# Gate and up products by seven block products for eight, down product in four phases

## Chip, cores and metric
The kernel runs on one NeuronCore of one Trainium2 chip. The metric is the device time of one execution, in microseconds (us); lower is better. TensorE multiplies, VectorE, ScalarE and GpSimd work elementwise, and the sync engine (SP) issues the DMA transfers.

## The reference
Two pre-norm layers, each a feed-forward block, a mixer (pooling and dilated attention) and a second feed-forward block, are followed by a third, different mixer and a fifth feed-forward block. Everything is float32, with 512 tokens, width 1024 and inner width 2816. Only the five feed-forward blocks change:

```python
def rmsnorm(x, g):
    xf = x.astype(jnp.float32)
    y = xf * lax.rsqrt(jnp.mean(xf * xf, axis=-1, keepdims=True) + NORM_EPS)
    return (y * g.astype(jnp.float32)).astype(x.dtype)

def swiglu(h, w_gate, w_up, w_down):
    return (jax.nn.silu(h @ w_gate) * (h @ w_up)) @ w_down
...
for l in range(DEPTH):
    x = x + 0.5 * swiglu(rmsnorm(x, ffn1_norm[l]), ffn1_w_gate[l], ffn1_w_up[l], ffn1_w_down[l])
    ...  # mixer
    x = x + 0.5 * swiglu(rmsnorm(x, ffn2_norm[l]), ffn2_w_gate[l], ffn2_w_up[l], ffn2_w_down[l])
```

## The kernel before
The residual `x` lies transposed in SBUF, eight tiles of 128 features by 512 tokens. Each float32 operand of a product is split into a high part, rounded to the fast format `float32r` by ScalarE (`ACT.activation(..., AF.Copy)`), and a low part, the remainder, which VectorE subtracts. `mm3` (line 255) then makes one 128-deep product of three matmuls: high by high, high by low, low by high (lines 257 to 259). Weights come in units of up to 128x1024, 512 KB: `load_unit` (line 224) issues the transfer from SP, `split_unit` (line 230) makes the high part `wh` (line 235) and the low part `wl` (line 237), and `unit()` keeps this two units ahead of the product. Raw and split tiles have three buffers each.

A feed-forward block is `ffn` (line 370). The activations are the split pairs `yh`, `yl` of the eight x tiles times the norm's gain (`split`, lines 293 and 294). The factor of the norm per token is taken out of the product: `square` adds up the squares (ScalarE, then GpSimd or VectorE, line 306), `row_factor` and `spread` make the factor `rbc`. For each of 22 blocks of the inner width, `one()` makes a gate block and an up block, 8 `mm3` of 512 columns each; `gate` (lines 376 to 384) scales both by `rbc` on VectorE, takes Silu on ScalarE, multiplies, and splits the result into `ah`, `al`. After all 22, the down product makes the eight x tiles one after another, 22 `mm3` each, and line 404 adds each to x and calls `nxt`, which prepares the next stage's pair. `two_first` makes the first two blocks of a layer with the last of the eight x tiles at the end, since it is the one that comes last.

Around the layers stand the mixers. The end of a mixer is `out_part(4, second)`: eight output tiles of 12 matmuls, each added to x and squared; `second` splits the first four tiles at once, and the last four are split behind the loop (lines 786 and 1250). The third mixer scales its output by a row factor first, through the tile `bt` (lines 1226 and 1227).

The order of instructions on each engine is set at build time: a list scheduler goes by the order of the program text and takes a later instruction first where an earlier one isn't ready by its own estimate. On the chip each engine then runs its list in order. Tiles of a pool that is opened in a `with` block lie where those of the pool closed before lay. The kernel has eight PSUM banks: six for products, two for transposes and row factors.

## Time and profile before

| | us |
|---|---|
| median of 3 runs | 2586.91 (2584.3 to 2588.48) |
| the profiled execution | 2587.41 |
| its span, first to last instruction | 2585.6 |
| TensorE busy in it | 2533.5 |
| VectorE busy in it | 1351.1 |
| mean granted clock of TensorE | 0.994 of full speed |

The profiled execution is one run with the hardware profiler on. An engine's busy time is the sum of its instructions; matmuls overlap in it, so the pace of a stream of matmuls is read from the starts in the timeline, not from their durations.

### The profile page before, as it was taken

Reading aid. Unit: us, or ns where it says so; the run is one execution under the profiler, and the core shown is the slowest. Engines: PE = TensorE matmul, PEld = TensorE weight load, DVE = VectorE, ACT = ScalarE, POOL = GpSimd, SP = SyncE. Lnnn points to the kernel's source line nnn. Section 1 sums busy time; section 2 is a strip of 40 time slices with the busy share of each in tenths; the row PEclk is TensorE's granted clock in tenths of the full one; section 3 lists DMA queues with packets and bytes.
Section 4 is the critical chain, followed back from the end, with each engine's and each line's share of the span. In section 5 each row is a group of like instructions: output and inputs, shape, how many; then the busy total and the mean of one; then the engine's idle time right before and its main releaser. Section 6 shows DMA issues by size and latency. Waiting matters only on the chain.

```text
span 2585.6 us, 31298 instructions
## 1 busy us (share of the span) xinstructions
PE 2533.5 (98%) x12114; PEld 2111.0 (82%) x12114; DVE 1351.1 (52%) x2235; ACT 1012.4 (39%) x1615; POOL 343.8 (13%) x498
## 2 busy tenths in 40 slices
PE   8999999999999999999999999999999999999997
PEld 6888888888888888888888888888887887788886
DVE  6444334786444334444336786444337787644423
ACT  4333223674333223332224674333235775432221
POOL 1000004431000000000004431000003553100000
PEclk9999999999999999999999999999999999999999
DMA  4333332112333333333332112333332311233332
GB/s 146 95 96 97 95 110 87 53 41 78 96 97 98 96 99 92 97 98 94 99 109 82 42 44 88 97 98 96 97 108 89 101 42 42 90 98 98 94 98 70
DMA packets 67542, 229.19 MB, mean 89 GB/s; under 512 B 8896, under 2 KB 9280, under 8 KB 67392
## 3 DMA queue, kind: packets, MB, share of 16 engines
q1 hardware_dynamic: 67392, 227.18, 29.0%
q8 instruction: 95, 1.56, 0.2%
q14 instruction: 55, 0.45, 0.1%
HBM read 225.06 MB, written 2.10 MB: 88 GB/s over the span
## 4 chain that ended last, share of the span: by engine, by line
PE 88%; DVE 6%; ACT 3%; issue 2%; POOL 1%; DMA 0%; SPq 0%; DVEq 0%; ACTq 0%; POOLq 0%
PE mm L257 27%; PE mm L259 27%; PE mm L258 27%; PE ov L751 1%; PE tp L733 1%; DVE wl L237 1%; PE mm L490 1%; PE mm L491 1%; PE ov L1030 1%; DVE qk L470 1%; ACT wh L235 1%; PE tp L1002 0%; DVE yl L294 0%; POOL win L610 0%; DVE qk L484 0%
## 5 line engine op out<-in xcount | busy, mean ns | idle before, releaser
L235 ACT ACTIVATE wh<-wr 128x1024 fp32r<-128x1024 f32 (+2 forms) x431 | 447.8, 1040 | 1218.5 <-PE mm L258 685.8
L257 PE MATMUL mm<-yh,wh 128*128 128x512 f32 x2008 | 787.7, 393 | 8.6 <-ACT wh L235 7.1
L258 PE MATMUL mm<-yl,wh 128*128 128x512 f32 x2008 | 783.7, 391 | 1.6 <-DVE yl L294 1.6
L259 PE MATMUL mm<-yh,wl 128*128 128x512 f32 x2008 | 783.1, 390 | 0.5 <-DVE wl L237 0.5
L237 DVE TENSOR_TENSOR wl<-wr,wh 128x1024 fp32r<-128x1024 f32 (+2 forms) x419 | 507.7, 1213 | 399.0 <-ACT wh L235 398.4
L257 PEld LDWEIGHTS mm<-yh,wh 128*128 128x128 f32 x2008 | 377.8, 188 | 85.6 <-ACT wh L235 7.1
L258 PEld LDWEIGHTS mm<-yl,wh 128*128 128x128 f32 x2008 | 378.0, 188 | 80.8 <-DVE yl L294 4.2
L259 PEld LDWEIGHTS mm<-yh,wl 128*128 128x128 f32 x2008 | 377.6, 188 | 79.4 <-DVE wl L237 1.2
L257 PE MATMUL mm<-ah,wh 128*128 128x512 f32 x880 | 342.3, 389 | 0.0
L258 PE MATMUL mm<-al,wh 128*128 128x512 f32 x880 | 342.3, 389 | 0.0
L259 PE MATMUL mm<-ah,wl 128*128 128x512 f32 x880 | 342.3, 389 | 0.0
L306 POOL TENSOR_TENSOR ss<-ss,sq 128x512 f32<-128x512 f32 x48 | 70.8, 1475 | 1726.0 <-ACT sq L305 1703.4
L379 DVE TENSOR_TENSOR t<-mm,rbc 128x512 f32<-128x512 f32 x110 | 76.1, 692 | 341.7 <-PE mm L259 341.7
L376 DVE TENSOR_TENSOR t<-mm,rbc 128x512 f32<-128x512 f32 x110 | 76.1, 692 | 235.7 <-PE mm L259 234.2
L258 PEld LDWEIGHTS mm<-al,wh 128*128 128x128 f32 x880 | 165.2, 188 | 34.4
L257 PEld LDWEIGHTS mm<-ah,wh 128*128 128x128 f32 x880 | 165.2, 188 | 34.4
L259 PEld LDWEIGHTS mm<-ah,wl 128*128 128x128 f32 x880 | 165.2, 188 | 34.1
L257 PE MATMUL mm<-wh,yh 128*128 128x256 f32 (+2 forms) x544 | 183.4, 337 | 1.0 <-DVE vhl L501 1.0
L259 PE MATMUL mm<-wh,yl 128*128 128x256 f32 (+2 forms) x544 | 176.0, 324 | 0.0
L258 PE MATMUL mm<-wl,yh 128*128 128x256 f32 (+2 forms) x544 | 175.7, 323 | 0.1
L257 PEld LDWEIGHTS mm<-wh,yh 128*128 128x128 f32 x544 | 104.1, 191 | 10.0 <-DVE vhl L501 1.9
L258 PEld LDWEIGHTS mm<-wl,yh 128*128 128x128 f32 x544 | 104.2, 192 | 8.6 <-DVE wl L237 0.5
(292 smaller groups left out, 2561.3 us busy)
## 6 DMA issues: line engine op xcount, KB each, us to landing
wr<-in_w SPq DMA_DIRECT2D x388, 512.0 KB, 3.5
wr<-in_w SPq DMA_DIRECT2D x40, 384.0 KB, 3.0
x<-in_xT SPq DMA_DIRECT2D x8, 256.0 KB, 5.8
out<-x SPq DMA_DIRECT2D x8, 256.0 KB, 2.0
bias<-in_consts SPq DMA_DIRECT2D x2, 448.0 KB, 4.2
wr<-in_w SPq DMA_DIRECT2D x2, 420.0 KB, 3.5
ws<-in_ws SPq DMA_DIRECT2D x2, 256.0 KB, 4.2
wr<-in_w SPq DMA_DIRECT2D x1, 280.0 KB, 2.8
```

Of the source, the lines that this page charges most:

```text
L235: ACT.activation(h[:, :n], r[:, :n], AF.Copy)
L237: state["low"] = eng.tensor_sub(l[:, :n], r[:, :n], h[:, :n].bitcast(F32)).ins
L257: PE.matmul(o, w[0], xx[0], start=start, stop=False)
L258: PE.matmul(o, w[0], xx[1], start=False, stop=False)
L259: PE.matmul(o, w[1], xx[0], start=False, stop=stop)
L306: eng.tensor_add(sums["s"], sums["s"], sq)
L376: V.tensor_mul(t1, g, rb)
L379: V.tensor_mul(t2, u, rb)
L470: return V.tensor_sub(dst, src, h.bitcast(F32))
L490: PE.matmul(o, q[g][:, cq], k[g][:, ck], start=True, stop=False)
L491: PE.matmul(o, q[g][:, cq], k[2 + g][:, ck], start=False, stop=True)
L733: PE.transpose(o[:, i * P : (i + 1) * P], prob[h * TC + i][0][:, j * P : (j + 1) * P], ident)
```

## The change
The inner width is taken in 11 pairs of 128-wide blocks. For each pair, with gate and up side by side in one weight tile of 1024, the product is a 2x2 block product: two halves of the depth (four x tiles each), two blocks of the inner width, two halves of the tokens (256 each). Instead of eight block products it makes seven (`PRODUCTS`), each 2 x 4 x 3 matmuls of 256 columns. Four of the seven weight tiles are sums (S1 to S4) that VectorE makes from raw tiles; on the side of x, `prep_a` makes a difference of token halves, and `prep_b` three further combinations. S2, S3 and W22 accumulate over W11's bank and S4 over S1's, with snapshots by ScalarE in between. `evac_act` and `evac` put the blocks together, and `finish` makes scaling, Silu, product and split of a block in three steps, spread over later products by `rest_of`. The pairs come in four phases of 2, 3, 3 and 3; the down product of a phase's blocks, eight pieces, is spread among the next phase's products, and each piece is added to x. The last phase's pieces come at the end, in the order 0, 4, 1, 5, 2, 6, 3, 7. The layer's pool holds weight buffers of its own, `wq` and `wd`, beside `wr`; it opens behind a mixer, where `layers` runs `prep_b` four times, and stays open from the second to the third layer. PSUM's six banks become three tags of two.

```diff
-DOWN = ((0, 8), (8, 8), (16, 6))
+PRODUCTS = ("W11", "S1", "S2", "W12", "S3", "S4", "W22")
+BLOCKS = {"W11": ((0, 0),), "S1": ((1, 0), (1, 1)), "W12": ((0, 1),)}
+PHASES = ((0, 1), (2, 3, 4), (5, 6, 7), (8, 9, 10))
+D_ORDER = (0, 4, 1, 5, 2, 6, 3, 7)
...
+        def source(j):
...
+            if name == "S1":
+                g["21"], g["22"] = m, m + 1
+                t = g["s1"] = state["ffn"].tile([P, 1024], F32, name="wt", tag="wt", bufs=2)
+                V.tensor_add(t, raws[m], raws[m + 1])
+                return t, 1024, []
+            if name == "S2":
+                t = g["s2"] = state["ffn"].tile([P, 1024], F32, name="wt", tag="wt", bufs=2)
+                V.tensor_add(t, g["s1"], raws[g["11"]])
+                return t, 1024, []
...
+            if name == "S3":
+                t = raws[g["21"]]
+                V.tensor_add(t, t, raws[g["11"]])
+                return t, 1024, [g["11"], g["21"]]
+            if name == "S4":
+                t = raws[g["12"]]
+                V.tensor_add(t, t, g["s2"])
+                return t, 1024, [g["12"]]
+            return raws[g["22"]], 1024, [g["22"]]
...
+        def prep_a(c, g):
+            t = small.tile([P, S], F32, name="sq", tag="sq", bufs=2)
+            ACT.activation(t, x[c], AF.Copy, scale=gain(g, c))
+            V.tensor_sub(t[:, HALF:], t[:, :HALF], t[:, HALF:])
+            h, l = new_pair(c)
+            ACT.activation(h, t, AF.Copy)
+            V.tensor_sub(l, t, h.bitcast(F32))
+
+        def prep_b(c, g):
+            b = state["ffn"].tile([P, 4, HALF], F32, name="b4", tag="cc", bufs=2)
+            r = state["ffn"].tile([P, 4, HALF], F32, name="r3", tag="cc", bufs=2)[:, :3]
+            ACT.activation(b[:, 0:2], x[c + 4], AF.Copy, scale=gain(g, c + 4))
+            ACT.activation(b[:, 2:4], x[c], AF.Copy, scale=gain(g, c))
+            V.tensor_sub(r[:, 1], b[:, 1], b[:, 3])
+            V.scalar_tensor_tensor(r[:, 0], r[:, 1], -1.0, b[:, 2], op0=ALU.mult, op1=ALU.subtract)
+            V.scalar_tensor_tensor(r[:, 2], r[:, 0], -1.0, b[:, 0], op0=ALU.mult, op1=ALU.subtract)
...
+            ACT.activation(h, r, AF.Copy)
+            yh, yl = new_pair(c + 4)
+            ACT.activation(yh, b[:, 0:2], AF.Copy)
+            V.tensor_sub(l, r, h.bitcast(F32))
+            V.tensor_sub(yl, b[:, 0:2], yh.bitcast(F32))
...
+            def evac(t, o):
+                if len(t) == 2:
+                    d = t[1]
                     V.scalar_tensor_tensor(x[d], o, coef, x[d], op0=ALU.mult, op1=ALU.add)
-                    nxt(d)
+                    if t[0] == len(PHASES) - 1:
+                        nxt(d)
+                    return
+                _, p, n = t
+                if n == "W12":
+                    V.tensor_add(flat(chunk(2 * p), 0), o[n], snap["W11"])
+                elif n == "S3":
+                    V.scalar_tensor_tensor(flat(chunk(2 * p + 1), 1), o[n], -1.0, snap["S1"], op0=ALU.mult, op1=ALU.subtract)
+                elif n == "S4":
+                    V.tensor_add(flat(chunk(2 * p), 1), o[n], snap["S2"])
+                    finish(2 * p)
+                elif n == "W22":
+                    finish(2 * p + 1)
...
+            def product(o, w, n, start):
+                for j in range(2):
+                    for c in range(4):
+                        m = 512 * j + c * P
+                        wh, wl = cut(w, slice(None), slice(m, m + P))
+                        xh, xl = operand(n, c)
+                        oo = o[:, j * HALF : (j + 1) * HALF]
+                        PE.matmul(oo, wh, xh, start=start and j == 0 and c == 0, stop=False, skip_group_check=True)
+                        PE.matmul(oo, wh, xl, start=False, stop=False, skip_group_check=True)
+                        PE.matmul(oo, wl, xh, start=False, stop=c == 3, skip_group_check=True)
...
+            for i, t in enumerate(ffn_plan()):
+                w = take()
...
+                if before:
+                    evac_act(*before)
+                highs(state["next"] + SPLIT)
+                if before:
+                    evac(*before)
+                rest_of()
+                lows(state["next"] + SPLIT)
+                before = now
+                if i == 2:
+                    r = row_factor(sums["s"], D, "rf")
+                if i == 3:
+                    got["rb"] = spread(r)
...
                     if d < 4:
-                        split(d, nxt)
+                        prep_a(d, nxt)
...
-                for c in range(4, KC):
-                    split(c, nxt)
...
+                if g is not None:
+                    for c in range(4):
+                        prep_b(c, g)
```

`highs` makes sums and high parts, `lows` the low parts, two products ahead.

## Rows read from the trace of the kernel before

**Rows 1.** The page, busy time and share of the span by engine.
```profile
PE 2533.5 (98%) x12114; PEld 2111.0 (82%) x12114; DVE 1351.1 (52%) x2235; ACT 1012.4 (39%) x1615; POOL 343.8 (13%) x498
```
**Rows 2.** The page, the chain that ended last, by line.
```profile
PE mm L257 27%; PE mm L259 27%; PE mm L258 27%; PE ov L751 1%; PE tp L733 1%; DVE wl L237 1%; PE mm L490 1%; PE mm L491 1%; PE ov L1030 1%; DVE qk L470 1%; ACT wh L235 1%; PE tp L1002 0%; DVE yl L294 0%; POOL win L610 0%; DVE qk L484 0%
```
**Rows 3.** Groups by form: shapes, count, busy us, mean ns, idle before.
```profile
L257 PE MATMUL mm<-yh,wh 128*128 128x512 f32 x2008 | 787.7, 393 | 8.6 <-ACT wh L235 7.1 <-ACT yh L293 1.5
...
L257 PEld LDWEIGHTS mm<-yh,wh 128*128 128x128 f32 x2008 | 377.8, 188 | 85.6 <-ACT wh L235 7.1 <-ACT yh L293 2.7 <-ACT yh L764 0.4
```
**Rows 4.** Timeline of TensorE in a down product: start, duration in us, instruction.
```profile
300.14 0.39 PE L257 MATMUL mm<-ah,wh 128*128 128x512 f32 x1
...
305.58 0.39 PE L257 MATMUL mm<-ah,wh 128*128 128x512 f32 x1
```
**Rows 5.** Windows: length, busy us by engine, granted clock, DMA share, GB/s.
```profile
30.00:264.00 234.00, 234.00 (x1036) 193.60 (x1035) 111.61 (x148) 72.19 (x90) 0.00 (x0) 1.00 0.32 97
...
599.00:613.00 14.00, 14.00 (x63) 11.59 (x62) 12.48 (x14) 9.40 (x16) 8.21 (x5) 1.00 0.27 82
613.00:626.00 13.00, 13.00 (x65) 10.87 (x64) 7.67 (x22) 4.73 (x7) 0.00 (x0) 1.00 0.22 75
...
2196.00:2209.00 13.00, 13.00 (x59) 10.60 (x57) 12.95 (x17) 7.32 (x12) 4.55 (x3) 1.00 0.19 69
2209.00:2216.00 7.00, 4.57 (x20) 3.28 (x19) 7.00 (x10) 4.77 (x8) 3.73 (x2) 1.00 0.25 75
...
8.00:18.00 10.00, 8.82 (x21) 5.45 (x20) 10.00 (x9) 6.27 (x11) 7.26 (x4) 1.00 0.82 300
18.00:30.00 12.00, 11.22 (x52) 9.10 (x53) 9.77 (x33) 3.12 (x4) 1.29 (x1) 1.00 0.27 72
...
2092.00:2096.00 4.00, 2.06 (x13) 1.52 (x12) 4.00 (x8) 1.97 (x6) 2.49 (x2) 0.94 0.55 171
2096.00:2104.00 8.00, 8.00 (x40) 7.16 (x40) 3.83 (x13) 3.48 (x10) 1.01 (x2) 0.61 0.10 38
```
**Rows 6.** Timeline of TensorE in a mixer, two streams of 256-column matmuls.
```profile
495.73 0.29 PE L259 MATMUL mm<-wh,yl 128*128 128x256 f32 x1
...
496.93 0.40 PE L490 MATMUL mm<-qk 128*128 128x512 f32 x1
...
506.91 0.28 PE L259 MATMUL mm<-wh,yl 128*128 128x256 f32 x1
...
508.10 0.40 PE L490 MATMUL mm<-qk 128*128 128x512 f32 x1
```
**Rows 7.** Timeline of the weight loads in the first of these streams.
```profile
495.38 0.19 PEld L257 LDWEIGHTS mm<-wh,yh 128*128 128x128 f32 x1
495.49 0.19 PEld L258 LDWEIGHTS mm<-wl,yh 128*128 128x128 f32 x1
```
**Rows 8.** Timeline of VectorE in a feed-forward layer, back to back.
```profile
103.93 0.69 DVE L380 TENSOR_TENSOR t<-t,t 128x512 f32<-128x512 f32 x1
104.54 1.22 DVE L237 TENSOR_TENSOR wl<-wr,wh 128x1024 fp32r<-128x1024 f32 x1
105.68 0.69 DVE L384 TENSOR_TENSOR al<-t,ah 128x512 fp32r<-128x512 f32 x1
...
272.00 0.74 DVE L294 SCALAR_TENSOR_TENSOR yl<-x,gains,yh 128x512 fp32r<-128x512 f32 x1
```
**Rows 9.** Groups by form on ScalarE.
```profile
L235 ACT ACTIVATE wh<-wr 128x1024 fp32r<-128x1024 f32 x388 | 411.4, 1061 | 1091.0 <-PE mm L258 577.6 <-issue 463.5 <-PE mm L259 40.2
L383 ACT ACTIVATE ah<-t 128x512 fp32r<-128x512 f32 x110 | 69.9, 636 | 75.6 <-DVE t L380 75.6
```
**Rows 10.** The tile `pw`: durations in ns (min/median/max), first and last start.
```profile
L470 DVE TENSOR_TENSOR pw<-sq,pw x2: 426/426/426, 381.4 to 1340.3; 128x256 fp32r<-128x256 f32 x2
```
**Rows 11.** Timeline at the end of the first layer, VectorE and SP.
```profile
375.13 0.69 DVE L404 SCALAR_TENSOR_TENSOR x<-mm,x 128x512 f32<-128x512 f32 x1 [1.94 <-PE mm L259]
375.13 0.33 SPq L550 DMA_DIRECT2D bias<-in_consts  x1
```

More of the change, by code (lines that the diff above doesn't have):

```diff
@@ L27 @@
 TC = S // P
+HALF = S // 2
 HD = 64
@@ new lines, in tile_blocks, with home @@
+        first_load = [0]
+        for _, ws in PLAN:
+            first_load.append(first_load[-1] + len(ws))
+        widths = [w for _, ws in PLAN for w in ws]
+        owner = [(j, k) for j, (_, ws) in enumerate(PLAN) for k in range(len(ws))]
+        HOMES = {"wr": 3, "wq": 3, "wd": 3}
+        raws, parts, made, open_ = {}, {}, {}, {h: [] for h in HOMES}
+        state = {"next": 0, "dma": 0, "add": 0, "split": 0, "spare": 0, "bank": 0, "pair": 0, "ffn": None}
+        def home(m):
+            j, _ = owner[m]
+            name = PLAN[j][0]
+            if name == "u":
+                return "wr"
+            if name in ("D", "W12"):
+                return "wd"
+            return "wq" if homes_of[j] % 2 else "wr"
@@ new lines, in tile_blocks, with group, high @@
+        groups = {}
+        def group(j):
+            while PLAN[j][0] != "W11":
+                j -= 1
+            return groups.setdefault(j, {})
+        def high(j):
+            if PLAN[j][0] not in ("u", "W11") and state["ffn"] is None:
+                return False
+            if not loads(j):
+                return False
+            src, n, free = source(j)
+            h = wspl.tile([P, 1024], F32R, name="wh", tag="wh")
+            ACT.activation(h[:, :n], src[:, :n], AF.Copy)
+            made[j] = src, n, free, h
+            return True
```

315 lines of the change are left out of this document (217 added, 98 removed).

## The prediction
> **What bounds the kernel now.** I read the page's busy shares first: TensorE is busy 98% of the span, VectorE 52%, ScalarE 39% [rows 1]. The chain of waits says the same by line: 27% each for lines 257, 258 and 259, the three matmuls of `mm3` [rows 2]. The groups by form show the unit of that work: 128x512 matmuls, six thousand of them on the activations `yh`, each with a 128x128 weight load of 188 ns [rows 3]. In the timeline of a feed-forward layer 24 such matmuls go from 300.14 to 305.58, so 0.2267 us from one start to the next [rows 4]; the loads lie beside them. The windows say how full the layer is: from 30 to 264 us TensorE is busy for all of 234 us, VectorE for 111.6 [rows 5]. So a feed-forward layer costs its matmuls, 1584 x 0.2267 = 359 us, and the other engines have half their time free there. Around the layers it is different: VectorE is busy 12.5 of 14 us before the second feed-forward layer, 12.95 of 13 before the last, and 10 of 10 at the start [rows 5].
>
> **What the change removes on TensorE.** Gate and up of a layer were 44 blocks x 24 = 1056 matmuls of 512 columns, 239.4 us. They become 11 pairs x 7 products x 24 = 1848 matmuls of 256 columns. The trace has that shape inside the mixer: ten steps from 506.91 to 508.10, 0.119 us each [rows 6]. 1848 x 0.119 = 219.9 us, so 19.5 us less per layer and **97 us** for five. The bounds of the step are half of 0.2267, 0.1134 (149 us in all), and 0.120, as in the neighbouring run of steps, 495.73 to 496.93 (88 us). I take 0.119: the same shape, the same loads. The down product keeps its 528 matmuls; only its order changes.
>
> The weight loads double in rate. In the mixer's run they start 0.11 us apart though each lasts 0.19 [rows 7], so they overlap each other and the matmuls, and I price them at nothing. The Trainium skill speaks against this: its page "TensorE: Matmul & The Clock Gate", Part 3, "The mechanism", says that a weight load overlaps with matmuls in flight only when it targets another group of rows of the array, which these full loads never do. The trace does not agree: loads of 0.19 us start 0.11 us apart. By that rule the 792 more loads of a layer would each add time and the change would lose; by the rows it wins 97 us. The rows decide, and what is left of the rule is a rival below.
>
> **What it adds on VectorE.** Back to back, a 512-wide operation steps 0.61 us and a 1024-wide one 1.14 [rows 8]; 768 wide I take halfway, 0.88. Per pair of blocks there were 4 weight remainders and 8 gate operations, 4 x 1.14 + 8 x 0.61 = 9.4 us in 21.8 of TensorE. Now there are 7 remainders, 4 block sums (S1 to S4) and 2 scalings by `rbc`, all 1024 wide, and 3 evacuations, 2 products and 2 remainders, 512 wide: 13 x 1.14 + 7 x 0.61 = 19.1 us in 7 x 2.856 = 20.0. The first phase has two pairs and no down product: 38.2 of 40.0, before the row factor. Later phases have 3 pairs and 8 down pieces (4 pieces of 128 deep, then 6): about 57 + 8 x 1.5 = 69 us in 60 + 8 x 4.08 = 93. So VectorE has no reserve in the first phase and 25% after it. The 24 further evacuations of `x` per layer are in this sum.
>
> Within a pair the work is uneven. Around W22 and the next W11 it is two sums, two remainders, two scalings, an evacuation and a product: 8.06 us in 5.71 of TensorE, 2.35 us behind. The remainder for S2, last in that queue, is due two products after W11 begins; VectorE gets there at 1.17 + 4.03 = 5.2 us of 5.7. Half a microsecond of slack, and the next five products win the 2.35 back. I price the 55 pairs at 0.2 us, **11 us**; the bounds are 0 and 2.35 x 55 = 129.
>
> ScalarE: 7 x 1.06 for the high parts and 8 x 0.6 for snapshots, Silu and copies [rows 9] is 12.3 us of 20.0: covered; W11's snapshot has S1's 2.86 us. If ScalarE ran late, S2, which accumulates over W11's bank, would wait. W22 waits likewise for the evacuation of S3 on VectorE, with the 2.86 us of S4 as cover. DMA: the same bytes, in 8 more transfers per layer. 97 GB/s flows in the layer now, and 300 was reached at the start [rows 5]; SP's queue holds only transfers, and tiles have three homes of three. Priced at nothing; with late homes S1, which needs two tiles, would wait first. GpSimd keeps its squares.
>
> **What it adds at the entries.** Four splits of x (0.74 us of VectorE each [rows 8]) become `prep_b`: three 256-wide operations (0.43 by the one row of that width [rows 10]), one of 768 and one of 512, 2.78 us. Four cost 11.1 in place of 3.0. `prep_a` costs 0.3 more than a split, 1.2 for four. Two block sums and a third remainder are wanted before S2: 3.4. Together **12.7 us** more of VectorE between the last output product and the end of S2.
> - After the first and second mixer: VectorE has 1.5 us free before 613 and some 3.7 of the next 9 [rows 5]; 7.5 us overhang. TensorE then waits, and after a wait of about 2 us (1.94 of the 4 from 2092) the trace shows the granted clock at a mean of 0.61 for 8 us, most of them at the 1.2 GHz level [rows 5]: 3.1 us. With 0.8 for the first phase, 11 each, **22**.
> - After the third mixer nothing is free (12.95 of 13), and the layer's tiles lie where the mixer's lay. A new pool opens when the old one is done: the mixer's `bias` was issued at 375.13, as the layer's last evacuation began [rows 11]. The mixer's `bt` is read until the last update of x, so all of `prep_b` comes after it: 1.3 + 1.4 for the first copies + 11.1 + 4.6 + 0.6 = 19 us against 8.6 of products, 10.4; with clock and first phase 14.4, less 2.4 that TensorE already loses there (4.57 busy of 7 [rows 5]). **12.**
> - At the start VectorE is full from 8 to 18 and has 2.2 us free to 30: 10.5, and with the first phase and later arrivals **12**.
> - From layer to layer the preparation runs beside eight down pieces, 32.6 us; VectorE's list there is 8 remainders 7.0, 8 evacuations 5.2, `prep_a` 4.2, `prep_b` 11.1, two square sums 1.2, the last pair's end 3.6 and the first three products' weights 5.7, 38 us against 32.6 + 8.6. Only the chain behind the last piece shows (0.69 + 1.4 + 1.4 + 0.9 + 1): **5**.
> Each of these is bounded by nothing, if the waits hide better than I stacked them, and by about twice the value, if both engines wait for each other in turn. From layer to mixer I price nothing: the last x tile is wanted 18 us into the first product. Behind the last layer the same chain follows.
>
> **The sum.** -97 + 11 + 22 + 12 + 12 + 5 = -35. The profiled execution took 2587.4 us (span 2585.6), 0.5 above the median of 2586.9. **2552 us.**
>
> **The rivals.**
> - *The entries hide.* VectorE's order lets block sums and remainders slip into gaps, and a third of the 51 us is paid, nothing in the pairs: 2587 - 97 + 17 = 2507, with some interior waits 2512. For it: idle VectorE in the layers [rows 5]. Against: VectorE is already full at the entries.
> - *The entries eat it all.* Each pays 1.7 times, as waits at half clock repeat: 2587 - 97 + 87 + 11 = 2588, no change. For it: the clock rows.
> - *The pair change turns TensorE into the waiter (slower).* The 2.35 us by which VectorE falls behind at W22 and W11 is not absorbed, since a remainder must wait for ScalarE's high part and every step passes between two engines. It costs up to 129 us over 55 pairs; it decides from (97 - 51) / 55 = 0.84 us per pair. At half, 2587 - 97 + 51 + 65 = 2606; in full 2670. For it: 19.1 of 20.0 in the first phase. Against: down pieces add slack in nine pairs of eleven.
> - *Weight loads are not covered.* If a 256-column stream ran at the load's own length of 0.188 us [rows 3], 1848 x 0.188 = 347 us per layer against 239: 108 x 5 = 540 us more, about 3127. The steps and starts of [rows 6, 7] speak against it. That is the outcome to which the rule of the Trainium skill quoted above points.
>
> **Chances and range.** My forecast 0.47 (own range 2520 to 2581), entries hidden 0.17, entries eat it 0.10, pair change 0.23, loads 0.03. So faster 0.64, same 0.10, slower 0.26, where 0.2%, 5 us, is about what can be told from no change here. The range reaches from 2507 (hidden entries) to 2615 (the pair change at half, with dearer entries); beyond lie the faster tail, full pair waits and the loads, 2 in 10.
>
> **What would show it.** The 256-column steps in the layers at 0.119 to 0.120 us; TensorE's idle time in clumps of 5 to 12 us behind each mixer and at the start, with VectorE full there and the granted clock near 0.5 behind them; between, windows of the later phases with TensorE busy throughout and VectorE at about 75 to 80%. Wrong: steps over 0.13; waits on the weight remainder or on S3's evacuation that recur every 20 us; waits for transfers; or entries without idle time.

## The result, and the profile after

2571.6 us (median of 4 runs, 2570.7 to 2572.9) against 2587.3 before (4 runs): a ratio of 0.9942, 95% interval 0.9924 to 0.9959. The change gains 15.7 us. 2552 was forecast, a gain of 35; the time lies inside the range, and the gain is less than half of what was worked out.

The page of the changed kernel, busy time and share by engine, then the chain by line, answer to [rows 1, 2]:

```profile
PE 2475.6 (96%) x16074; PEld 2248.3 (87%) x16074; DVE 2003.3 (78%) x2935; ACT 1345.3 (52%) x2120; POOL 343.9 (13%) x498
...
PE 84%; DVE 10%; ACT 3%; issue 2%; POOL 1%; DMA 0%; DVEq 0%; SPq 0%; ACTq 0%; POOLq 0%
PE x L629 14%; PE x L630 14%; PE x L628 14%; PE dn L404 8%; PE dn L405 7%; PE dn L406 7%; PE mm L404 4%; PE mm L405 4%; PE mm L406 4%; DVE wl L368 2%; PE ov L1015 2%; PE tp L997 2%; PE mm L754 1%; PE mm L755 1%; PE ov L1292 1%
```

TensorE is busy for 58 us less than before [rows 1], and its idle time went from 52 us (the span of 2585.6 less 2533.5) to 95.5. VectorE rose from 52% to 78% in the share of the span, and has 10% of the chain. So the gain was made and given back in waits. Two timelines tell of the gain: TensorE's in the middle of a layer (start, duration, instruction), and its weight loads there:

```profile
300.07 0.28 PE L628 MATMUL x<-rh,wh 128*128 128x256 f32 x1
300.19 0.28 PE L629 MATMUL x<-rl,wh 128*128 128x256 f32 x1
...
300.79 0.28 PE L628 MATMUL x<-yh,wh 128*128 128x256 f32 x1
...
300.07 0.19 PEld L629 LDWEIGHTS x<-rl,wh 128*128 128x128 f32 x1
300.19 0.19 PEld L630 LDWEIGHTS x<-rh,wl 128*128 128x128 f32 x1
```

The 256-column step is 0.120 us, six steps in 0.72, with loads of 0.19 us that start 0.12 apart. A layer's gate and up products take 1848 x 0.120 = 221.8 us in place of 239.4: 17.6 us less, 88 in five layers. Where the rest went is read from the ends of the layers, the start of the last matmul of each down product in the two traces:

| layer | before | after | later by, since the layer before | given back (this + 17.6) | forecast |
|---|---|---|---|---|---|
| 1 (with the start) | 374.7 | 375.5 | +0.8 | 18.4 | 12 |
| 2 (behind the first mixer) | 973.7 | 974.9 | +0.4 | 18.0 | 11 |
| 3 (behind layer 2) | 1334.2 | 1321.6 | -13.7 | 3.9 | 5 |
| 4 (behind the second mixer) | 1933.1 | 1917.7 | -2.9 | 14.7 | 11 |
| 5 (behind the third mixer) | 2569.7 | 2555.0 | +0.7 | 18.3 | 12 |

The sum is 73 us given back of 88. All of it lies in the first pair of each layer. From a layer's first matmul to that of its eighth product the trace has 45.8, 38.0, 25.0, 37.4 and 47.4 us, where seven products alone are 20.2. From the eighth product to the layer's end it has 321.5 to 322.0 us, and the work there is 70 x 2.88 + 528 x 0.2267 = 321.3: nothing is lost behind the first pair. The windows show both (length, busy us by engine, granted clock, DMA share, GB/s), as [rows 5] did:

```profile
100.00:370.00 270.00, 270.00 (x1823) 250.88 (x1822) 205.93 (x226) 125.84 (x165) 5.48 (x5) 1.00 0.31 93
615.00:624.00 9.00, 6.57 (x51) 6.08 (x49) 9.00 (x12) 5.71 (x10) 3.21 (x2) 1.00 0.00 0
624.00:640.00 16.00, 9.09 (x35) 6.97 (x36) 15.83 (x33) 9.06 (x14) 0.00 (x0) 0.57 0.22 66
640.00:645.00 5.00, 5.00 (x32) 5.00 (x31) 2.81 (x4) 1.96 (x2) 0.00 (x0) 0.66 0.10 18
2200.00:2219.00 19.00, 11.14 (x45) 9.81 (x46) 18.86 (x36) 10.43 (x16) 0.00 (x0) 0.59 0.39 133
```

Between 100 and 370 us TensorE is busy for all of 270, VectorE for 76%. Behind the first mixer, from 624 to 640, TensorE is busy for 9.1 of 16 and VectorE for 15.83, and the granted clock's mean is 0.57. What VectorE does there is the core of this case. The timeline of VectorE, with two additions of GpSimd (POOL) in it:

```profile
607.73 2.31 DVE L326 TENSOR_TENSOR wt<-wr 128x1024 f32<-128x1024 f32 x1
...
610.90 1.86 DVE L330 TENSOR_TENSOR wt<-wt,wr 128x1024 f32<-128x1024 f32 x1
...
614.66 2.25 POOL L476 TENSOR_TENSOR ss<-ss,sq 128x512 f32<-128x512 f32 x1 [2.98 <-ACT sq L475]
...
615.69 1.78 DVE L435 TENSOR_TENSOR yl<-sq,yh 128x512 fp32r<-128x512 f32 x1
...
617.65 1.30 POOL L476 TENSOR_TENSOR ss<-ss,sq 128x512 f32<-128x512 f32 x1 [0.74 <-ACT sq L475]
...
617.99 1.25 DVE L444 SCALAR_TENSOR_TENSOR r<-r,b 128x256 f32<-128x256 f32 x1
...
620.36 0.68 DVE L959 TENSOR_TENSOR x<-mm,x 128x512 f32<-128x512 f32 x1
620.96 0.41 DVE L445 SCALAR_TENSOR_TENSOR r<-r,b 128x256 f32<-128x256 f32 x1
...
623.90 1.21 DVE L337 TENSOR_TENSOR wr<-wr 128x1024 f32<-128x1024 f32 x1
...
626.31 1.21 DVE L368 TENSOR_TENSOR wl<-wd,wh 128x1024 fp32r<-128x1024 f32 x1
...
627.78 1.21 DVE L368 TENSOR_TENSOR wl<-wr,wh 128x1024 fp32r<-128x1024 f32 x1
...
629.86 1.21 DVE L341 TENSOR_TENSOR wd<-wd,wt 128x1024 f32<-128x1024 f32 x1
...
632.33 1.21 DVE L326 TENSOR_TENSOR wt<-wq 128x1024 f32<-128x1024 f32 x1
...
633.87 1.21 DVE L330 TENSOR_TENSOR wt<-wt,wq 128x1024 f32<-128x1024 f32 x1
...
635.95 1.21 DVE L337 TENSOR_TENSOR wq<-wq 128x1024 f32<-128x1024 f32 x1
...
639.87 0.95 DVE L450 TENSOR_TENSOR rl<-r,rh 128x768 fp32r<-128x768 f32 x1
```

The last x update is at 620.36, and S2, the third product, needs the last remainder `rl` of the four preparations, which ends at 640.8. In these 20 us VectorE rests for 0.2, but much of what it executes is not needed yet: S3's sum at 623.90, S3's remainder at 627.78, S4's sum at 629.86, and three block sums of the next pair at 632.33, 633.87 and 635.95. With W12's remainder (626.31) that is seven operations that S2 does not want, stepping 1.14 us, 8.0 us. And beside GpSimd's sums some operations last longer than usual: 1.78 in place of 0.68, 1.25 in place of 0.41, 2.31 and 1.86 in place of 1.21.

TensorE's waits from 612 to 650 us are 9.5 in all. The longest single one is that of S2's first matmul for W11's snapshot on ScalarE (us in total, times, longest):

```profile
PE x L628 <- ACT snap L557: 2.4, 1, 2.4
```

The end of the waiting stands in TensorE's timeline:

```profile
638.15 0.58 PE L629 MATMUL x<-yl,wh 128*128 128x256 f32 x1 [1.02 <-DVE yl L451]
...
641.52 0.41 PE L629 MATMUL x<-rl,wh 128*128 128x256 f32 x1
...
643.43 0.28 PE L629 MATMUL x<-rl,wh 128*128 128x256 f32 x1
```

TensorE's list mixes matmuls of W12 with those of S2, so its last wait is for the last `yl`, which `prep_b` makes just ahead of the last `rl`. From 638.15 on it has no gap, but its steps are 0.21 us (641.52 to 643.43 are nine), the 1.2 GHz level, and the last `rl`, ready at 640.82, is read at 641.52. At 0.120 us a step the matmul at 643.43 could have started some 1.5 us earlier, an estimate: 0.7 us until `rl` is read, and 9 x 0.09.

### The profile page after: what moved, and what is told of

Read it like the earlier page. It is cut to its first block, busy times and chain, and to the rows that moved or that the text cites. A ratio compares the mean times of both kernels' runs of the same rounds, so it can differ in the third digit from the quotient of the medians.

```text
span 2571.1 us, 40560 instructions
## 1 busy us (share of the span) xinstructions
PE 2475.6 (96%) x16074; PEld 2248.3 (87%) x16074; DVE 2003.3 (78%) x2935; ACT 1345.3 (52%) x2120; POOL 343.9 (13%) x498
## 4 chain that ended last, share of the span: by engine, by line
PE 84%; DVE 10%; ACT 3%; issue 2%; POOL 1%; DMA 0%; DVEq 0%; SPq 0%; ACTq 0%; POOLq 0%
PE x L629 14%; PE x L630 14%; PE x L628 14%; PE dn L404 8%; PE dn L405 7%; PE dn L406 7%; PE mm L404 4%; PE mm L405 4%; PE mm L406 4%; DVE wl L368 2%; PE ov L1015 2%; PE tp L997 2%; PE mm L754 1%; PE mm L755 1%; PE ov L1292 1%
## 5 line engine op out<-in xcount | busy, mean ns | idle before, releaser
L628 PE MATMUL x<-yh,wh 128*128 128x256 f32 x1760 | 507.1, 288 | 20.2 <-ACT wh L360 14.1
L629 PE MATMUL x<-yl,wh 128*128 128x256 f32 x1760 | 506.8, 288 | 13.6 <-DVE yl L435 7.9
L630 PE MATMUL x<-yh,wl 128*128 128x256 f32 x1760 | 505.7, 287 | 3.7 <-DVE wl L368 3.7
L628 PE MATMUL x<-rh,wh 128*128 128x256 f32 x1320 | 377.2, 286 | 14.8 <-ACT rh L447 10.0
L629 PE MATMUL x<-rl,wh 128*128 128x256 f32 x1320 | 376.9, 286 | 4.0 <-DVE rl L450 4.0
L630 PE MATMUL x<-rh,wl 128*128 128x256 f32 x1320 | 376.0, 285 | 0.8 <-DVE wl L368 0.8
L628 PEld LDWEIGHTS x<-yh,wh 128*128 128x128 f32 x1760 | 344.2, 196 | 25.8 <-ACT wh L360 14.8
L629 PEld LDWEIGHTS x<-yl,wh 128*128 128x128 f32 x1760 | 344.3, 196 | 19.9 <-DVE yl L435 9.7
L630 PEld LDWEIGHTS x<-yh,wl 128*128 128x128 f32 x1760 | 344.7, 196 | 4.9 <-DVE wl L368 4.9
L404 PE MATMUL dn<-ah,wh 128*128 128x512 f32 x880 | 343.9, 391 | 0.0
L368 DVE TENSOR_TENSOR wl<-wd,wh 128x768 fp32r<-128x768 f32 (+2 forms) x270 | 276.4, 1024 | 42.8 <-ACT wh L360 40.2
L628 PEld LDWEIGHTS x<-rh,wh 128*128 128x128 f32 x1320 | 255.4, 193 | 19.6 <-ACT rh L447 12.1
```

Source lines behind the costliest of these rows:

```text
L368: state["low"] = eng.tensor_sub(l[:, :n], src[:, :n], h[:, :n].bitcast(F32)).ins
L404: PE.matmul(o, w[0], xx[0], start=start, stop=False)
L628: PE.matmul(oo, wh, xh, start=start and j == 0 and c == 0, stop=False, skip_group_check=True)
L629: PE.matmul(oo, wh, xl, start=False, stop=False, skip_group_check=True)
L630: PE.matmul(oo, wl, xh, start=False, stop=c == 3, skip_group_check=True)
```

## The experiments

Times are medians; each stands beside 2571.6 of the changed kernel. "First pairs" are the five stretches from a layer's first matmul to its eighth product, as above; behind them the layers take 321 to 324 us in all runs. The kernel before took 2585 to 2587 us beside these runs, so a difference of 2 us between two runs says little.

| run | us | ratio to before, 95% | first pairs 1 to 5 |
|---|---|---|---|
| changed kernel | 2571.6 | 0.9924 to 0.9959 | 45.8, 38.0, 25.0, 37.4, 47.4 |
| e3, down pieces clumped | 2570.9 | 0.9931 to 0.9961 | 45.0, 37.8, 25.0, 37.6, 47.5 |
| e9, more VectorE work | 2590.1 | 1.0004 to 1.0023 | 46.8, 42.4, 26.2, 42.5, 51.4 |
| e18, remainders repeated | 2583.9 | 0.9986 to 1.0005 | 46.2, 37.8, 27.5, 38.0, 46.7 |
| e1, own buffers | 2562.3 | 0.9894 to 0.9924 | 47.6, 32.0, 27.3, 32.2, 41.5 |
| e2, sums behind | 2559.5 | 0.9885 to 0.9914 | 43.3, 32.0, 27.0, 32.3, 42.9 |
| e6, both | 2561.8 | 0.9892 to 0.9921 | 46.0, 32.4, 26.9, 32.4, 40.1 |
| e4, differences late | 2569.8 | 0.9926 to 0.9959 | 45.1, 36.1, 25.4, 35.9, 46.8 |
| e7, no differences | 2525.7 | 0.9753 to 0.9782 | 38.4, 23.0, 21.7, 22.8, 35.6 |
| e16, remainder twice | 2596.3 | 1.0027 to 1.0057 | 53.0, 41.7, 27.5, 41.6, 52.5 |
| e10, no squares | 2545.7 | 0.9829 to 0.9858 | 38.5, 32.8, 21.6, 32.9, 41.7 |
| e20, sums on TensorE | 2576.7 | 0.9953 to 0.9979 | 44.8, 31.6, 26.8, 31.7, 42.7 |
| e19, e2 and e20 | 2563.8 | 0.9897 to 0.9930 | 43.2, 27.0, 29.4, 26.5, 38.9 |
| e14, filled wait | 2580.2 | 0.9965 to 0.9986 | 45.8, 39.9, 27.7, 40.1, 47.4 |

### The pairs: is VectorE's reserve what hides the unevenness? (e3, e9, e18)

e3 puts the down pieces in a clump:

```diff
-                if (j + 1) * len(todo) // len(ds) == i + 1:
+                if (2 if j < 7 else 20) == i:
```


> Seven of a phase's eight down pieces stand together behind the third product of the next phase, where the changed kernel spreads them over its 21 products; the eighth stays at the phase's end. The same work otherwise. It tests the rival of the prediction that TensorE becomes the waiter in the pairs: a pair alone is 20.2 us of TensorE, and a down piece adds 2.0 to 4.1 us in which VectorE has one eviction only. If the spread pieces give VectorE the time that it needs (the rival's price, up to 2.35 us for each of the some 45 pairs that lose their pieces), the time rises by 50 to 106 us, to 2620 to 2677, and TensorE shows gaps at each pair. If VectorE fits into 20.2 us without them, it stays within 2566 to 2582, with gaps only at the clumps, where three to seven evictions in place of one stand in a row.

2570.9, and first pairs and rests as in the changed kernel. The spread pieces are not what keeps VectorE in step: a pair alone, 20.2 us of TensorE, is enough.

e9 adds VectorE work at the feared place, in `evac` behind W22's `finish`, on a tile that GpSimd fills at each layer's start:

```diff
+                    if t[0]:
+                        for _ in range(4):
+                            V.tensor_mul(more, more, more)
```


> Four more VectorE operations, 1024 wide, on a tile of their own, behind the evacuation of W22 in every pair of the second to fourth phase (45 pairs, 1.14 us each, 4.6 us a pair): VectorE falls 2.35 + 4.6 = 6.9 us behind at the place that the forecast feared. The result is the same. If the half microsecond of slack that the forecast worked out there were right, each pair would lose some 4 us, 180 in all, about 2750. If VectorE's reserve over a pair and its down pieces counts (19.1 + 4.6 of 20.2 + 8.2 to 16), nothing: 2566 to 2580. Between: two products of lead (5.7 us) cover most of it and 1.2 us a pair show, 54 in all: about 2625.

18.5 us more. But behind the first pairs the layers still take 321.5 to 322.7 us. The loss stands at the entries (the second, fourth and fifth first pairs 4 to 5 us longer). Part of the added work runs there too: nothing waits for it, and the order of VectorE's list let it slip. Behind the first mixer e9's timeline has one multiplication among the updates of x, 2.00 us long, and four in the first pair; the fifth layer's first pair has seven.

```profile
602.94 2.00 DVE L618 TENSOR_TENSOR more<-more 128x1024 f32<-128x1024 f32 x1
...
645.84 1.22 DVE L618 TENSOR_TENSOR more<-more 128x1024 f32<-128x1024 f32 x1
```

GpSimd's fill of the tile, by contrast, ended at 599.87, before its sums of the squares began. TensorE's longest wait there is 5.2 us for S1's weight remainder, which VectorE comes to later than in the changed kernel. How much of the loss is the added work and how much the changed order is not separated. e18 adds as much without a new tile, in `finish`:

```diff
-                    V.tensor_sub(hl[1], g, hl[0].bitcast(F32))
+                    for _ in range(5 if f > 3 else 1):
+                        V.tensor_sub(hl[1], g, hl[0].bitcast(F32))
```


> In the changed kernel the remainder of each activation block from the second phase on is computed five times in place of once, with the same result: 8 operations of 0.61 us, 4.9 us more of VectorE per pair, without a new buffer and without work for GpSimd. The run with 4.6 us more per pair lost 18.5 us, all of it at the entries and none in the pairs by its trace, which had a fill of a new tile on GpSimd at each entry. If the pairs absorb it and that fill was the cost, 2569 to 2577. If the reserve of the pairs is used up, 45 pairs show it: 2600 and more.

2583.9, between the two expectations. The layers behind their first pair take 323.4 to 324.3, some 2 us more each, 10.4 in all: 0.23 us a pair for 4.9 us of work. The window from 100 to 370 us in e9 and e18:

```profile
100.00:370.00 270.00, 270.00 (x1827) 251.03 (x1826) 232.46 (x252) 125.80 (x165) 5.39 (x4) 1.00 0.31 93
```

```profile
100.00:370.00 270.00, 269.18 (x1815) 249.24 (x1814) 243.45 (x296) 123.30 (x163) 5.86 (x4) 1.00 0.30 93
```

VectorE goes to 86% and 90% there, and TensorE waits for 0 and 0.8 of 270 us. So the price of the pair change is nothing, and not for lack of work at W22: the half microsecond of slack that the forecast found in it was wrong.

### The entries: a chain, or VectorE's amount? (e1, e2, e6, e4, e7, e16)

e1 gives the scaled copies of `prep_b` their own buffers:

```diff
-            b = state["ffn"].tile([P, 4, HALF], F32, name="b4", tag="cc", bufs=2)
+            b0, b1 = (state["ffn"].tile([P, 2, HALF], F32, name=f"b{e}", tag=f"a{e}", bufs=12) for e in "hl")
...
```


> The preparation of each of the four row pairs in prep_b takes its scaled copies b from the two buffers that it shares with r3, so copy c+1 waits until chain c is through; here the copies get buffers of their own (the ones the activation pieces use later), nothing else changes. Theory A, a serial chain through two shared buffers: the period of the chain, 6.0 us in the second layer of the changed kernel (r3 pieces of line 443 at 625.04, 630.99, 637.09), falls towards the 3.6 us of its own work, and some 4 to 8 us go from the entry of each layer behind a mixer: 2571.6 becomes 2540 to 2556. Theory B, VectorE has more work in the entry than time, whatever its order: the chain's copies run earlier on ScalarE but the VectorE part ends when it did; 2568 to 2575. Theory C, what stands in front of the chain on VectorE is work that nobody needs yet: the copies come earlier, the period stays near 6 us; 2562 to 2573.

e2 queues S3 and S4 of the first group, and all sums of later groups, behind the last instruction of `prep_b`:

```diff
+            state["hold"] = V.tensor_sub(yl, b[:, 0:2], yh.bitcast(F32)).ins
...
-                V.tensor_add(t, t, raws[g["11"]])
+                with held():
+                    V.tensor_add(t, t, raws[g["11"]])
```

where `held` is `tc.issue_after(state["hold"])` once that instruction is there.

> The block sums S3 and S4 of a layer's first group and the sums of the groups after it are queued on their engine behind the last instruction of prep_b, where the changed kernel has them between its instructions; the same instructions otherwise. Theory A (buffers): the chain's period stays at 6 us, no gain, 2568 to 2578, and a little loss where S3 is now late. Theory B (VectorE's total): S3 and S4 are needed for the first group, so they only swap places: 2566 to 2576. Theory C (work that nobody needs yet ahead of the chain): five operations of 1.14 us leave the stretch 624 to 640 of the second layer, up to 5.7 us an entry, at four or five entries: 2543 to 2560.

e6 is both:

> Both earlier edits together: the copies of prep_b in buffers of their own, and the block sums that are needed later queued behind the last instruction of prep_b. Alone they took 9 and 12 us from the changed kernel (2562.3 and 2559.5 against 2571.6), at the entries only. If they remove the same wait (the chain through two buffers is slow because of what stands in it, or the other way round), together they give 2556 to 2561. If they remove different waits, 2548 to 2554. If only VectorE's total counts now, no more than the better one alone: 2558 to 2561.

2562.3, 2559.5 and 2561.8. Each takes 9 to 12 us off, both together no more. VectorE's timeline in e1 and then in e2, behind the first mixer, tells why:

```profile
620.58 0.68 DVE L959 TENSOR_TENSOR x<-mm,x 128x512 f32<-128x512 f32 x1
...
633.55 0.94 DVE L450 TENSOR_TENSOR rl<-r,rh 128x768 fp32r<-128x768 f32 x1
...
641.86 1.22 DVE L326 TENSOR_TENSOR wt<-wq 128x1024 f32<-128x1024 f32 x1
```

```profile
617.08 0.68 DVE L968 TENSOR_TENSOR x<-mm,x 128x512 f32<-128x512 f32 x1
...
631.74 0.96 DVE L459 TENSOR_TENSOR rl<-r,rh 128x768 fp32r<-128x768 f32 x1
...
637.75 1.22 DVE L332 TENSOR_TENSOR wt<-wq 128x1024 f32<-128x1024 f32 x1
```

From the last x update to the end of the last `rl` it is 20.5 us in the changed kernel (620.36 to 640.82), 13.9 in e1 and 15.6 in e2. In both the next pair's sums now stand behind (L326 at 641.86, L332 at 637.75). An engine's order is not the program's: with the copies made earlier, e1's preparation came to stand before those sums. So e1 and e2 remove the same wait, and that is Theory C, work that nobody needs yet ahead of the preparation. The buffers as such are not shown to matter.

e4 lets the first pair run the products that need no differences first:

```diff
+FIRST = ("W11", "S1", "W12", "S4", "S2", "S3", "W22")
...
+        todo = [(ph, p, n) for p in pairs for n in (PRODUCTS if p else FIRST)]
```


> The first pair of each layer runs its products in the order W11, S1, W12, S4, S2, S3, W22: those that need the three differences of prep_b come last, where the changed kernel has the first of them as its third product. The same products and sums; S2 is evicted onto S4's sum in place of the other way round, and S2, S3 and W22 of that pair, which share a bank, now stand in a row. Theory A and C (the entry waits for the chain's last preparation, which the products of the other kind can cover): two products more, 5.8 us, lie beside the chain in each of four entries; less about 2 us at five for the bank in a row: 2555 to 2563. Theory B (VectorE's total): the stretch ends when VectorE is done, and the bank in a row costs: 2570 to 2580. W12 and S4 need the plain second half yh and yl, which is the last thing that prep_b makes: if that, not the differences, ends the wait, it is as for theory B.

2569.8. S2, S3 and W22 share a bank in a row here, so what is taken of S2 and of S3 holds the product behind it too, and its values differ; the amount of work is the same. Two products more beside the preparation gave 2 us, where theories A and C expected 9 to 17: W12 then waits for the last `yl`, which `prep_b` makes beside the last `rl` (TensorE's last wait behind the first mixer is 0.81 us for `yl`). This is the case that the expectation's last sentence names.

e7 leaves the differences out, e16 makes their remainder twice:

```diff
-            b = state["ffn"].tile([P, 4, HALF], F32, name="b4", tag="cc", bufs=2)
...
-            V.tensor_sub(yl, b[:, 0:2], yh.bitcast(F32))
+            split(c + 4, g)
+            rest[c] = pair[c + 4]
```
```diff
             V.tensor_sub(l, r, h.bitcast(F32))
+            V.tensor_sub(l, r, h.bitcast(F32))
```


> The three differences of prep_b, their high and low parts and the scaled copies are left out: prep_b is the one split per row block that the kernel before had, and S2, S3 and W22 take that split's halves in place of the differences, so the values differ and the TensorE work is the same. It measures what the preparation costs at the entries. Theory A (prep_b's chain sets the entry): first pairs of the second, fourth and fifth layers fall from 37 to 47 us to 25 to 30, and the time to 2510 to 2535. Theory B (VectorE's rest, the sums, remainders and squares, is late by itself): 2545 to 2562. The forecast's own terms put the preparation at 8.1 of the 12.7 us that VectorE gets more at an entry, so two thirds of 73 us of entry losses, 49, would go: 2523.

> In the changed kernel the remainder of the three differences (768 wide, 0.95 us) is computed twice in prep_b, with the same result: 3.8 us more of VectorE at each entry, on no chain. It doubles the suspected cost. If the entry lasts as long as VectorE's work ahead of the last difference, four entries pay 3.8 us each or more (the last remainder is then also later) and the third layer's little or none: 2585 to 2597. If a chain of waits between the engines sets the entry and VectorE has gaps in it, 2571 to 2577.

2525.7: 46 us less, of 49 expected, and the first pairs behind the first two mixers fall to 23 us (behind the third to 35.6, where 25 to 30 was expected). 2596.3: 24.7 us more for five entries x 3.8 us, so 1.3 us for each microsecond put in, as a mean; behind the first two mixers the first pairs grew by 3.7 and 4.2. e16's timeline, from the last x update to the remainder that S2 waits for, with the matmul that waits:

```profile
625.54 0.68 DVE L960 TENSOR_TENSOR x<-mm,x 128x512 f32<-128x512 f32 x1
...
648.90 0.96 DVE L450 TENSOR_TENSOR rl<-r,rh 128x768 fp32r<-128x768 f32 x1 [0.91 <-ACT rh L447]
...
650.79 0.95 DVE L451 TENSOR_TENSOR rl<-r,rh 128x768 fp32r<-128x768 f32 x1
...
651.79 0.39 PE L630 MATMUL x<-rl,wh 128*128 128x256 f32 x1 [0.20 <-DVE rl L451]
```

It is now 26.2 us (to 651.74), where it was 20.5. But the repeated remainder is not "on no chain", as its expectation had it: it writes `rl` again, TensorE waits for it (651.79), and it reads `r`, whose buffer the next preparation needs. So e16 cannot tell a chain between two engines from VectorE's amount of work. e2 can: it leaves the preparation and its buffers as they are and only moves other work behind it, and the stretch falls from 20.5 to 15.6 us. Over all runs with differences, behind the first mixer, the last `rl` ends 15 to 31 us after the layer's first matmul, and the eighth product begins 10 to 14 us after that; only in e17, below, it is 21.5. What VectorE executes until the last `rl` sets the entry. Whether the 4.0 us from one `rl` to the next that are left in e2 are a chain through the shared buffers stays open: e6 gave the copies their own buffers, and the order on VectorE changed with them.

### GpSimd's sums beside it (e10, e11, e12, e15, e20, e19)

e10 leaves seven of eight squares out at each entry:

```diff
-            square(x[c], c == 0, V if c >= KC - 2 else G)
+            if c == 0:
+                square(x[c], True)
...
```

> The squares of x ahead of the feed-forward layers are left out but for the first row block, so the row factor is another and the values differ: seven squares on ScalarE, five sums on GpSimd and two on VectorE less at each entry. It measures whether GpSimd's sums beside VectorE's operations, which stretch these (the sum behind L337 lasted 2.31 us in place of 1.23), make the entries dear. Theory D (they do): first pairs of the second, fourth and fifth layers 5 to 8 us shorter, 2545 to 2556. Theories A and C (the chain in prep_b): only the two sums and a few stretched operations go, 1 to 3 us an entry, 2560 to 2570.

2545.7, 26 us less: more than the two sums on VectorE (1.4 us an entry) can explain. The traces show where. Behind the first mixer the last x update follows the mixer's last product by 0.4 us in e10, by 4.8 in the changed kernel; from there to the end of the last `rl` it is 19.6 against 20.5. So the squares make VectorE late ahead of the last update: from 601 to 620 us it rests for 0.9, and the four stretched operations shown above last 3.7 us longer than usual. ScalarE waits there too, 5.7 us in five waits for GpSimd's sums, since the squares and the copies of `prep_a` share two buffers `sq`; with VectorE so full these waits hardly decide, but no run separates them.

Three tries followed to keep the squares and move them. e11 calls them behind `prep_b` in the program and takes the row factor two products later; e12 is e11 with e2; e15 is e12 with the squares asked for behind `prep_b` in the queues:

```diff
-                    square_x(d)
...
+                    with tc.issue_after(state["hold"]):
+                        for c in range(KC):
+                            square_x(c)
```


> All the squares of x ahead of a feed-forward layer are made behind prep_b in place of beside the mixer's updates and prep_a, and the row factor is taken two products later (its first user comes behind S4). Nothing is left out. If GpSimd's sums cost because VectorE's operations stretch beside them while TensorE waits for these, and because two sums stand on VectorE there, most of the 26 us that leaving the squares out gave come without leaving anything out: 2548 to 2558. If it is the amount of work in the entry, wherever it stands, the first pair only loses them later: 2566 to 2574.

> The late squares and the block sums queued behind the last instruction of prep_b, together. Theory B in its new form: TensorE waits for whatever VectorE executes ahead of the last difference, each microsecond of it for one microsecond and a bit (the half clock behind the wait), so work that is moved behind it adds up: the 12 us of the sums and what the late squares give, 2538 to 2548. If both moves remove the same wait, no better than the better of the two.

> As the run with late squares and sums behind, but the squares ahead of the three layers that follow a mixer, with the one ahead of the third layer, are really queued behind the last instruction of prep_b (in the run before, the order of the engines still had them in front: sums of line 485 at 605.05, 607.08 and 609.94). If TensorE waits for whatever VectorE executes ahead of the last difference, stretched or not, the gain of leaving the squares out (26 us) and that of the sums (12) now add up in good part: 2538 to 2550. If the squares only cost because they are work, wherever it stands, 2556 to 2564.

2576.2, 2560.6 and 2562.5: no gain over the same kernel without the move (2571.6 and 2559.5). They did not test what they were meant to: in all three traces GpSimd's additions still stand in front, as in e15 from 609.74 to 614.70 (below, in the last section); only VectorE's two sums moved in e15, to 628.89 and 631.50, the first of them still ahead of the last `rl`. e20 removes them in another way: TensorE sums the squares.

```diff
+                PE.matmul(sums["o"][:, i : i + 1], t[:, i * P : (i + 1) * P], ones,
+                          start=k == 1 and i == 0, stop=k == KC, skip_group_check=True)
```


> In the changed kernel the squares of x ahead of the layers behind a mixer and of the third layer are summed by TensorE, four matmuls of one column for each row block into one bank (0.25 us each in the row factor of the changed kernel), in place of five additions on GpSimd and two on VectorE; the first layer keeps its sums. Nothing is left out. VectorE loses two operations and the stretch beside GpSimd, some 5 us an entry, for 8 us of TensorE, most of it in its waits. If VectorE's time ahead of the last difference sets the entry, 2549 to 2560 (three to four of the five entries, of the 26 us without squares). If GpSimd's sums were harmless, 2571 and more by the new matmuls, up to 2600.

> The block sums behind the last instruction of prep_b and the squares summed by TensorE, together: two different pieces of VectorE's time ahead of the last difference. If that time sets the entry, the 12 us of the sums and the gain of the other add up: 2538 to 2550. If what is left is the chain between ScalarE and VectorE, or TensorE's own added matmuls, 2554 to 2564, no better than the sums alone.

By their times, 2576.7 and 2563.8, both fall where the other reading was expected (GpSimd's sums harmless; no better than the sums alone). The first pairs say otherwise. Behind the first and the second mixer e20 has 31.6 and 31.7, against 38.0 and 37.4; e2 has 32.0 and 32.3; together, in e19, 27.0 and 26.5. The two moves add up, 11.0 us of 6.4 and 6.0, as work on one queue does. A part of e20's 6.4 may be that its layer begins later; but the last x update follows the mixer's last product by 0.8 us in it, much as in e10, which has no new matmuls. What eats the gain is TensorE itself, in a timeline of e20 among the mixer's last products:

```profile
602.35 0.40 PE L406 MATMUL mm<-yh,wl 128*128 128x512 f32 x1
602.59 0.95 PE L443 MATMUL tst<-ones,sp 128*128 128x1 f32 x8
603.40 0.48 PE L404 MATMUL mm<-yh,wh 128*128 128x512 f32 x1
```

One row block's four matmuls of one column are eight instructions and hold TensorE for 0.81 us: 8 x 0.81 = 6.5 us at each of four entries, 26 us, most of it where TensorE had no wait: the stretches between a layer's last matmul and the next layer's first grew by 17 us in sum.

### The clock behind the wait (e14, e13, e17)

e14 fills the wait ahead of the third product with 48 matmuls on an idle bank:

```diff
+                    if i == 2 and state.pop("fill", 0):
+                        od = tbank("dn")
+                        for _ in range(48):
+                            PE.matmul(od[:, :HALF], pair[0][0][:, :P], pair[0][0][:, :HALF], start=True, stop=True)
```


> In the changed kernel, 48 matmuls of 256 columns on an idle bank (5.8 us at full clock, their result is used by nothing) are put ahead of the third product of the first pair in the first, second, fourth and fifth layers, where TensorE waits for the preparation. The waits stay; TensorE is busy in part of them. It measures what the clock behind the waits costs. If the granted clock of 0.57 and 0.66 behind the wait is what makes an entry dear, the products behind the wait (5.0 and 4.4 us in place of 2.9) come back to 2.9 to 3.3 and 2 to 4 us go at each of four entries: 2556 to 2564. If the time is VectorE's alone, since the next products wait for it too, 2568 to 2575.

> The late squares, the sums behind, and the 48 matmuls that fill the wait. If what is left of the wait is still longer than 6 us, the fill adds its gain to the two moves, 2 to 3 us an entry: 2530 to 2540. Where the wait has become shorter than the fill, the fill stands in the way and the time is longer than without it: 2545 to 2555.

```profile
624.00:640.00 16.00, 11.93 (x72) 10.43 (x70) 14.60 (x27) 8.04 (x13) 0.00 (x0) 0.79 0.21 66
640.00:645.00 5.00, 3.79 (x20) 3.39 (x21) 3.58 (x10) 1.51 (x2) 0.00 (x0) 0.80 0.34 104
```

The granted clock is 0.79 and 0.80 here, where the same windows had 0.57 and 0.66, and the time is 8.5 us longer, outside both expected ranges. e13 adds the fill to e12: 2559.2 against 2560.6, nothing, and outside its ranges too. But e14 does not price the clock, since the fill changed VectorE's order as well:

```profile
639.84 0.69 DVE L606 TENSOR_TENSOR cc<-x,snap 128x512 f32<-128x512 f32 x1 [1.40 <-PE x L630]
...
641.96 0.95 DVE L450 TENSOR_TENSOR rl<-r,rh 128x768 fp32r<-128x768 f32 x1
```

The evacuation of W12 now stands ahead of the last `rl` and waits 1.40 us for TensorE, and the last `rl` ends 23.0 us after the last x update in place of 20.5. TensorE's steps are 0.21 us again from 633 to 639. What the half clock costs stays open; the rows of the changed kernel above give an estimate of 1.5 us for the entry behind the first mixer.

e17 joins e15 with e1's buffers:

> The squares held, the sums behind and the copies of prep_b in buffers of their own. The buffers gave nothing on top of the sums (2561.8 against 2559.5). If VectorE's amount sets the entry, nothing again: within 3 us of the run without them. If, with squares and sums gone, the chain's two buffers (4.1 us a step against 2.9 of VectorE's own) are what is left, 4 to 10 us less.

2574.2, 12 us worse than e15. All of `rl` is done by 631.3, but TensorE's waits from 610 to 650 us now name another engine:

```profile
PE x L637 <- ACT snap L566: 11.4, 1, 11.4
```

W11's snapshot, which S2 must follow in its bank, runs at 630.04 on ScalarE. Its queue had stood at a square that waited for a buffer until GpSimd's sum was done:

```profile
627.10 0.63 ACT L484 ACTIVATE sq<-x 128x512 f32<-128x512 f32 x1 [3.67 <-POOL ss L485]
```

On VectorE the remainders of the weights for S1 and S2 came only behind the last `rl` (631.78). One order mended, another broken.

The fastest version is e2: 2559.5 us, a ratio of 0.9885 to 0.9914 to the kernel before.

## Why the prediction fell short

- **The step on TensorE** was right in kind, and 0.120 us in place of 0.119, its named bound: 88 us, not 97.
- **Weight loads priced at nothing**: right, at twice their rate. The Trainium skill, "TensorE: Matmul & The Clock Gate", Part 3, "The mechanism", says that a load overlaps matmuls in flight only when it targets another group of rows. This trace does not agree with that sentence: full loads of 0.19 us start 0.12 us apart through whole layers.
- **Pairs, 11 us**: nothing was paid. e3, e9 and e18 show that several microseconds a pair are absorbed. That the slack of half a microsecond came from listing VectorE's work in one assumed order is likely, but not shown.
- **Entries, 51 us: measured 73. This is the step that failed**, and in it the sentence "Two block sums and a third remainder are wanted before S2: 3.4". It counted what S2 wants. What decides is what VectorE executes before S2's last operand, and seven more operations, 8.0 us, stood there that S2 does not want, with operations stretched beside GpSimd ("GpSimd keeps its squares" had no price). The same seven stand behind the third mixer: from its last x update to the end of the last `rl` it is 27.2 us, where the forecast worked out 19. At the start there are four of them. e2 and e19 take 6 and 11 us off the second layer's first pair by moving and removing just these; e16 shows a price of 1.3 us, as a mean, for each microsecond added.
- **The half clock, 3.1 us of each entry behind a mixer**: not settled. The rows behind the first mixer give an estimate of 1.5; e14's fill changed VectorE's order too and prices nothing.
- **From layer to layer, 5 us**: 3.9. There the down pieces cover the list, as worked out.
- **DMA and S3's evacuation at nothing**: no wait of TensorE in the changed kernel names either.
- **ScalarE at nothing**: not right at the entries. "W11's snapshot has S1's 2.86 us" did not hold there: behind the first two mixers S2's first matmul waits 2.4 us for it. Little of this counts, since S2's first `rl` was ready only 0.75 us before that matmul began; in e17 the same wait became the longest.

With the measured terms the sum is -88 + 0 + 73 = -15. That the time missed by 20 us only is in part luck: the step missed by 9 and the entries by 22, and the 11 us of the pairs, which were not paid, took back a third of that. Of the rivals, "the entries eat it all" named the right place, 1.4 times the entries in place of its 1.7, but by another mechanism: it had waits at half clock that repeat.

## What to carry to other kernels

When work moves to an engine that is full for a stretch, count everything that its queue executes ahead of the awaited result, not only what the result needs; work that is only ready early belongs behind it. Moving a call in the program is not moving it in the queue where the order follows readiness: read the changed trace before believing the experiment. An average reserve of a quarter hides much inside a steady loop and nothing at its entry.

## What was not expected of the hardware

VectorE's operations stretch beside GpSimd's additions by their operands. In e15's timeline, GpSimd and then VectorE, behind the first mixer:

```profile
609.74 4.96 POOL L485 TENSOR_TENSOR ss<-ss,sq 128x512 f32<-128x512 f32 x3 [1.36 <-ACT sq L484]
...
612.03 1.51 DVE L453 SCALAR_TENSOR_TENSOR r<-r,b 128x256 f32<-128x256 f32 x1
613.47 0.68 DVE L968 TENSOR_TENSOR x<-mm,x 128x512 f32<-128x512 f32 x1
614.07 0.92 DVE L454 SCALAR_TENSOR_TENSOR r<-r,b 128x256 f32<-128x256 f32 x1
```

The difference of two SBUF tiles takes 1.51 and 0.92 us in place of 0.42; the x update between them, with one operand in PSUM, its usual 0.68. The Trainium skill, "SBUF — State Buffer", "Who interferes with whom", says that a VectorE instruction with two SBUF inputs contends with a GpSimd instruction that reads SBUF; these rows agree. And a 256-column step costs 0.120 us where half of the 512-column step is 0.113: from the two rows, an estimate of 0.013 us for each matmul of these two widths (0.2267 = a + 512 b, 0.120 = a + 256 b). The 792 more matmuls of a layer cost 10.5 us by it, 53 in five layers, out of the 141 that the fewer columns are worth.
